# Small parameter rows and the forget gate's columns loaded on POOL's queue; every low part of w_in and u made on DVE

## The chip, the core and the metric

One core of one Trainium2 chip runs one launch of the kernel. The metric is the device time in microseconds (us), lower is better. The engines named below are PE (TensorE, matrix products), DVE (VectorE), ACT (ScalarE), POOL (GpSimd) and SP (SyncE, which here only starts transfers); transfers can be started by SP, ACT and POOL and are carried out by 16 DMA engines.

## What is computed (the reference)

One layer of a decoder on 512 tokens of width 1024: an adaLN-modulated input goes through one projection into two mixers (attention with forget gates, and a gated linear recurrence, RG-LRU), then an output projection, then a mixture of 16 experts. Cut to what the change touches:

```
mod = silu(c) @ w_ada + b_ada                  # (1, 6144): shift, scale, gate, twice
u   = layer_norm(x) * (1 + sc_m) + sh_m        # (512, 1024)
proj = u @ w_in                                # (512, 2568): q, k, v, forget logits, xb, gb
attn = forgetting_attention(q, k, v, f_logit + b_f)
lru  = rg_lru_branch(xb, gb, conv_w, conv_b, w_rg, b_rg, w_ig, b_ig, lru_lambda)
mix  = concat(rms_norm(attn), rms_norm(lru)) @ w_out
x = layer_norm(alpha * x + (1 + gt_m) * mix, ln1_g, ln1_b)
x = layer_norm(alpha * x + (1 + gt_f) * moe(layer_norm(x) * (1 + sc_f) + sh_f), ln2_g, ln2_b)
```

All of it is float32. The kernel makes a float32 product from three faster ones: each operand is split into a high part (a cast to a shorter float type, on ACT) and a low part (operand minus high part, a subtraction), and `mm3` adds high*high, low*high and high*low in PSUM (lines 101 to 103).

## The kernel before

The program is one long list of steps. PE's and SP's instructions run in the order in which they are written; those of ACT, DVE and POOL are ordered by a scheduler that looks at what each step needs, and each engine then runs its list strictly in order. A transfer is an instruction in the list of the engine that starts it. The completion of transfers is counted on a few shared semaphores: eight (DMAHW0 to 7) for transfers that SP and ACT start, eight others (DMASW0 to 7) for those of POOL. They are handed out in turn, so a transfer that takes up a semaphore first waits until the one that last used it has landed.

The start of the program, up to the projection:
- c (line 166) is loaded and turned into `cb` (line 247). ACT starts the four quarters of one w_ada block, `ws2` (line 175), then `wf`, the 32 columns of w_in that hold the forget gate's (line 391, 1024 pieces of 128 bytes), then eleven loads of small parameter rows into `v64` (lines 177 to 183). SP starts the four tiles of x (line 218), then the w_ada blocks ws0, ws3 and ws1 (line 252) with the first blocks of w_in (`wi`, line 355) between them. POOL starts `bfc` (line 185) and four loads of the recurrence's gate weights `bdr` (lines 416, 417).
- `lnx` normalizes one tile of x: statistics on DVE (line 331), the reciprocal root on POOL (line 326), the normalization on DVE (line 346), then eight transposes on PE (line 350) whose results DVE and ACT copy into `xnT` (line 351). v64 is transposed as well (line 422) and copied to `vt`.
- `ada_part` multiplies c with a w_ada block (line 265, result copied by ACT to `part`, line 267), `ada_T` turns it into columns (line 318), from which DVE makes `sc1T` (line 323) and `shT` (line 321), the scale and shift of one half of the features.
- `u_half(g)` applies scale and shift to four of eight feature blocks (DVE, line 383) and splits the result into `uh` (ACT, line 384) and `ul` (line 385). `f_half` multiplies with wf (line 396), `proj_half` a first or second half of one w_in block.

w_in comes in 20 blocks of 128 columns: eight for the recurrence (columns 1544 to 2567: four `xb`, four `gb`), then four of v, then q and k. `win_load` loads one (line 355), makes its high part `whi` on ACT (line 357) and its low part `wlo` (line 358). The pairs rotate through four buffers, so the fifth block's `whi` waits until PE has used the first block. For the recurrence's blocks 3 to 8 POOL makes the low part, for all others DVE. Three blocks are begun (`NPRE_ = 3`) while the second half of u is being made; then `proj()` finishes them, the convolution of each follows on DVE (`xc`, lines 551 and 553, split on ACT and DVE into `xch` and `xcl`), and `lru_gates` multiplies it with the gate weights on PE. Later `lru_ss` adds the squares of the recurrence's output: three additions on POOL (line 623), then four products with a column of ones (line 626).

The experts' weights are loaded by SP at line 817 into buffers that earlier stages free; their matmuls fill the second half of the program.

## Time and profile before

| | |
|---|---|
| time, median of 3 runs | 678.32 us (672.58 to 680.26) |
| the profiled execution | 675.8 us, its span 674.1 us |
| PE busy | 601.3 us, 89% of the span |
| DVE, ACT, POOL busy | 463.9, 322.7, 200.4 us |
| mean granted clock of PE | 0.956 of full speed |

The span runs from the first to the last instruction. Share of time over the whole span says little here, since PE is busy nearly all the time from about 36 us on, and waits in the first 36 us and at a few seams. The views that follow are the waits (for each engine and line, who ended its idle time: total, times, longest), the timeline (start, length, engine, line, what is written from what, and in brackets the idle time before it and its releaser) and the stretches (busy time of each engine, granted clock of PE and share of the DMA engines in a window).

### The profile page before, as it was taken

To read this page: it belongs to the slowest core of one execution; us is meant where nothing else is said; L and a number is where in the kernel's file an instruction comes from. 1 tells how busy PE (TensorE), PEld (TensorE's weight loads), DVE (VectorE), ACT (ScalarE), POOL (GpSimd) and SP (SyncE) were. 2 spreads that over 40 slices of the span, in tenths; PEclk is the share of its full clock that TensorE was granted. 3 is DMA by queue.
4 is the path that set the end of the run, shared out by engine and by line. 5 is a ranking of instruction groups with operands and counts; after the bars stand their busy time and mean duration, and the time that the engine had idled before them with its cause. 6 is when DMAs were issued, how large, how long until landed. Compare 5 with 4: busy or idle time off the path is not lost.

```text
span 674.1 us, 10228 instructions
## 1 busy us (share of the span) xinstructions
PE 601.3 (89%) x3537; PEld 444.4 (66%) x3537; DVE 463.9 (69%) x731; ACT 322.7 (48%) x508; POOL 200.4 (30%) x188
## 2 busy tenths in 40 slices
PE   1687999999995999998899999999999999999960
PEld 0444777777775887888877776666667677676440
DVE  5747869954346577779698675947695876985075
ACT  0324597334234436655286464635455564562070
POOL 5436202300000000033044353535354444443013
PEclk9899899999996999997989999999999989999795
DMA  8994317797445403184789988799989999799503
GB/s 266 339 264 149 101 29 253 235 267 253 156 158 189 154 1 125 64 298 159 261 289 361 389 288 300 287 316 351 351 300 337 368 371 362 277 381 384 207 10 118
DMA packets 91394, 164.61 MB, mean 244 GB/s; under 512 B 10169, under 2 KB 30761, under 8 KB 91340
## 3 DMA queue, kind: packets, MB, share of 16 engines
q1 hardware_dynamic: 83796, 149.02, 63.3%
q0 software_dynamic: 4624, 10.52, 6.0%
q10 hardware_dynamic: 2920, 4.39, 1.9%
q8 instruction: 29, 0.48, 0.3%
q14 instruction: 25, 0.20, 0.1%
HBM read 155.54 MB, written 12.39 MB: 249 GB/s over the span
## 4 chain that ended last, share of the span: by engine, by line
PE 63%; DVE 13%; DMA 8%; issue 6%; ACT 5%; POOL 3%; ACTq 0%; DVEq 0%; POOLq 0%; SPq 0%
PE ps L102 12%; PE ps L101 12%; PE ps L103 12%; PE ps L1416 7%; PE ps L1432 3%; DVE wlo L810 2%; DMA er<-in_w_e_down_dram 2%; DMA x2d<-y,ix 2%; DMA er<-in_w_e_gate_dram 1%; POOL wlo L810 1%; DMA wf<-in_w_in_dram 1%; DVE tail L1751 1%; PE ps L881 1%; PE ps L318 1%; PE ps L1032 1%
## 5 line engine op out<-in xcount | busy, mean ns | idle before, releaser
L810 DVE TENSOR_TENSOR wlo<-er,whi 128x1024 fp32r<-128x1024 f32 x91 | 147.5, 1638 | 28.1 <-ACT whi L809 28.0
L809 ACT CAST whi<-er 128x1024 fp32r<-128x1024 f32 x120 | 125.3, 1050 | 70.3 <-PE ps L103 62.4
L810 POOL TENSOR_TENSOR wlo<-er,whi 128x1024 fp32r<-128x1024 f32 x29 | 74.1, 2554 | 77.8 <-ACT whi L809 77.6
L101 PE MATMUL ps<-uh,whi 128*128 128x512 f32 x160 | 65.0, 406 | 0.0
L102 PE MATMUL ps<-ul,whi 128*128 128x512 f32 x160 | 62.9, 393 | 0.0
L103 PE MATMUL ps<-uh,wlo 128*128 128x512 f32 x160 | 62.9, 393 | 0.0
L1416 PE MATMUL ps<-er,xT 128*64 128x256 f32 x512 | 61.1, 393 | 0.0
L102 PE MATMUL ps<-wlo,xth 128*128 128x512 f32 x144 | 57.3, 398 | 4.0 <-POOL wlo L810 2.7
L101 PE MATMUL ps<-whi,xth 128*128 128x512 f32 x144 | 58.4, 406 | 0.0
L103 PE MATMUL ps<-whi,xtl 128*128 128x512 f32 x144 | 57.0, 396 | 1.2 <-DVE xtl L98 1.2
L326 POOL TENSOR_TENSOR rA<-rA,nhalf 128x1 f32<-128x1 f32 x4 | 2.2, 549 | 166.3 <-DVE rA L915 166.3
L1416 PEld LDWEIGHTS ps<-er,xT 128*64 128x64 f32 x512 | 36.4, 141 | 21.9 <-issue 6.1
L101 PEld LDWEIGHTS ps<-uh,whi 128*128 128x128 f32 x160 | 30.5, 191 | 12.5 <-issue 3.0
L102 PE MATMUL ps<-wlo,hth 128*128 128x512 f32 x80 | 32.6, 407 | 2.5 <-DVE wlo L810 2.5
L102 PEld LDWEIGHTS ps<-wlo,xth 128*128 128x128 f32 x144 | 27.1, 188 | 11.5 <-POOL wlo L810 4.5
L102 PEld LDWEIGHTS ps<-ul,whi 128*128 128x128 f32 x160 | 30.4, 190 | 6.5 <-issue 0.5
L103 PEld LDWEIGHTS ps<-uh,wlo 128*128 128x128 f32 x160 | 30.3, 190 | 6.6
L101 PE MATMUL ps<-whi,hth 128*128 128x512 f32 x80 | 33.0, 412 | 0.0
L103 PEld LDWEIGHTS ps<-whi,xtl 128*128 128x128 f32 x144 | 27.1, 188 | 7.8 <-DVE xtl L98 1.6
L103 PE MATMUL ps<-whi,htl 128*128 128x512 f32 x80 | 32.2, 402 | 0.0
L357 ACT CAST whi<-wi 128x1024 fp32r<-128x1024 f32 x20 | 20.9, 1047 | 22.1 <-DMA wi<-in_w_in_dram 15.5
L101 PEld LDWEIGHTS ps<-whi,xth 128*128 128x128 f32 x144 | 27.1, 188 | 5.6
(406 smaller groups left out, 1279.2 us busy)
## 6 DMA issues: line engine op xcount, KB each, us to landing
er<-in_w_e_gate_dram SPq DMA_DIRECT2D x64, 512.0 KB
er<-in_w_e_up_dram SPq DMA_DIRECT2D x64, 512.0 KB
er<-in_w_e_down_dram SPq DMA_DIRECT2D x64, 512.0 KB
wa<-in_w_ada_dram SPq DMA_DIRECT2D x44, 512.0 KB
wi<-in_w_in_dram SPq DMA_DIRECT2D x20, 512.0 KB
wo<-in_w_out_dram SPq DMA_DIRECT2D x8, 512.0 KB
wa<-in_w_ada_dram ACTq DMA_DIRECT2D x4, 512.0 KB
x<-in_x_dram SPq DMA_DIRECT2D x4, 512.0 KB
```

The lines of the kernel that those rows point to most:

```text
L101: T.matmul(o, l[0], r[0], start=start, stop=False)
L102: T.matmul(o, l[0], r[1], start=False, stop=False)
L103: T.matmul(o, l[1], r[0], start=False, stop=stop)
L318: T.matmul(p[:, b:b + 1], part[:, b * 128:(b + 1) * 128], s4 if sel_ is None else sel_, start=True, stop=True)
L357: A.copy(hl[0], r)
L809: A.copy(hl[0], r)
L810: (eng or V).tensor_sub(hl[1], r, hl[0].bitcast(F32))
L881: T.transpose(p[:, n, j, :], src[:, kb * 128:(kb + 1) * 128], ident)
L1032: T.matmul(pls[qi], yTs[qi][k // 4][:, k % 4, :], wr[:, k, :], start=k == 0, stop=k == 7)
L1416: T.matmul(p[64 * h:64 * h + 64, :], xT[:, k, :], ws[w0 + k // 2][:, k % 2, h * 256:(h + 1) * 256], start=k == 0, stop=k == 7)
L1432: T.matmul(py[64 * h:64 * h + 64, :], hT[:, k % 2, (k // 2) * 64:(k // 2) * 64 + 64], ws[8 + k][:, h * 512:(h + 1) * 512], start=k == 0, s ...
L1751: return lambda: V.scalar_tensor_tensor(ys[t][:, hs[h]], ys[t][:, hs[h]], d["r", t], g2[:, hs[h]], op0=OP.mult, op1=OP.mult)
```

## The change

1. The eleven loads into v64 and the load of wf are started by POOL instead of ACT.
2. All low parts of w_in blocks, and all low parts of u, are made on DVE: POOL loses six of 128 by 1024 and two of 128 by 512.
3. Both products `ada_part(ws3)` and `ada_part(ws1)` are issued before either `ada_T`.
4. `lru_ss` makes two additions on POOL, not three; the fourth square goes through PE, which makes eight products, not four.

```
@@ small parameters
-    A.dma_start(v64[0:8], ln1_g.rearrange("o (k p) -> (o k) p", p=128))
-    A.dma_start(v64[80:88], ln1_b.rearrange("o (k p) -> (o k) p", p=128))
+    G.dma_start(v64[0:8], ln1_g.rearrange("o (k p) -> (o k) p", p=128))
+    G.dma_start(v64[80:88], ln1_b.rearrange("o (k p) -> (o k) p", p=128))
...
     for r0, src in ((40, conv_b), (44, b_rg), (48, b_ig), (52, lru_lambda), (56, g_attn), (60, g_lru)):
-        A.dma_start(v64[r0:r0 + 4], src.rearrange("o (k p) -> (o k) p", p=128))
-    A.dma_start(v64[24:40], conv_w.rearrange("o w (k p) -> (o w k) p", p=128))
+        G.dma_start(v64[r0:r0 + 4], src.rearrange("o (k p) -> (o k) p", p=128))
+    G.dma_start(v64[24:40], conv_w.rearrange("o w (k p) -> (o w k) p", p=128))
@@ win_load
-        (V if c0 in LOV or not whl else G if 1536 <= c0 else V).tensor_sub(hl[1], r, hl[0].bitcast(F32))
+        V.tensor_sub(hl[1], r, hl[0].bitcast(F32))
@@ u_half
-            (G if k in (5, 7) else V).tensor_sub(ul[:, k, :], xnT[:, k, :], uh[:, k, :].bitcast(F32))
+            V.tensor_sub(ul[:, k, :], xnT[:, k, :], uh[:, k, :].bitcast(F32))
@@
-    A.dma_start(wf, w_in[0, :, 1536:1568].rearrange("(k p) n -> p k n", p=128))
+    G.dma_start(wf, w_in[0, :, 1536:1568].rearrange("(k p) n -> p k n", p=128))
@@
-    ada_T(3, ada_part(ws3))
-    ada_T(1, ada_part(ws1))
+    part3, part1 = ada_part(ws3), ada_part(ws1)
+    ada_T(3, part3)
+    ada_T(1, part1)
@@ lru_ss
-        for i in range(1, 4):
+        for i in (1, 2):
             G.tensor_add(lb[:, 0, :], lb[:, 0, :], lb[:, i, :])
         ssL = ps([128, 4])
         for t in range(NT):
-            T.matmul(ssL[:, t:t + 1], lb[:, 0, t * 128:(t + 1) * 128], ones1, start=True, stop=True)
+            for i in (0, 3):
+                T.matmul(ssL[:, t:t + 1], lb[:, i, t * 128:(t + 1) * 128], ones1, start=i == 0, stop=i == 3)
```

The order of the instructions moves at three places. SP's first transfers, with the semaphore that each waits for; x_190 to x_193 are the four tiles of x, wa_216 is the first quarter of ws0. Before:

```order
L218 DMA x_190<-in_x_dram 128x1024
L218 DMA x_191<-in_x_dram 128x1024 [waits DMAHW4_49]
L218 DMA x_192<-in_x_dram 128x1024 [waits DMAHW5_49]
L218 DMA x_193<-in_x_dram 128x1024 [waits DMAHW1_49]
L252 DMA wa_216<-in_w_ada_dram 128x2x512 [waits DMAHW5_49]
```

And now:

```order
L218 DMA x_190<-in_x_dram 128x1024
L218 DMA x_191<-in_x_dram 128x1024
L218 DMA x_192<-in_x_dram 128x1024
L218 DMA x_193<-in_x_dram 128x1024 [waits DMAHW0_49]
L252 DMA wa_216<-in_w_ada_dram 128x2x512 [waits DMAHW1_49]
```

DMAHW4 was the semaphore of wf; DMAHW0 and 1 are those of the first two quarters of ws2. The second and third tile of x now wait for nothing.

POOL's list from its first transfer to the first reciprocal root (rs_280). Before:

```order
L185 DMA bfc<-in_b_f_dram 8x1
L210 MEMSET mneg_178 128x128
L414 MEMSET bdr_254 128x512
L211 AFFINE_SELECT mneg_178<-mneg_178 128x128 [waits Pool_49]
L416 DMA bdr_254<-in_w_rg_dram 64x4x64 [waits Pool_49]
L417 DMA bdr_254<-in_w_rg_dram 64x4x64
...
L1026 TENSOR_TENSOR keybT<-keybT,ecol 16x1 [waits Pool_49]
L326 TENSOR_TENSOR rs_280<-ve_278,nhalf 128x1 [waits DVE_49]
```

And now; ahead of the first row stand the first eight loads into v64, which wait for nothing, and the "..." hides the last two of them:

```order
L182 DMA v_145<-in_g_attn_dram 4x128 [waits DMASW0_49]
...
L185 DMA bfc<-in_b_f_dram 8x1 [waits DMASW3_49]
L210 MEMSET mneg_178 128x128
L391 DMA wf<-in_w_in_dram 128x8x32 [waits DMASW4_49]
L211 AFFINE_SELECT mneg_178<-mneg_178 128x128 [waits Pool_49]
L414 MEMSET bdr_254 128x512
L414 MEMSET bdr_258 128x512
L416 DMA bdr_254<-in_w_rg_dram 64x4x64 [waits DMASW5_49,Pool_49]
L417 DMA bdr_254<-in_w_rg_dram 64x4x64 [waits DMASW6_49]
L416 DMA bdr_258<-in_w_ig_dram 64x4x64 [waits DMASW7_49,Pool_49]
L417 DMA bdr_258<-in_w_ig_dram 64x4x64 [waits DMASW0_49]
L326 TENSOR_TENSOR rs_280<-ve_278,nhalf 128x1 [waits DVE_49]
```

Seventeen transfers stand ahead of rs_280 where five stood, and from the ninth on each waits for an earlier one to land. DVE's list moves with it: its four casts of mneg (line 214), which need the AFFINE_SELECT, and the statistics of all four tiles of x now stand ahead of the first normalization (line 346).

DVE's list from the gate weights' low parts (bdl) to the low part of the first convolution (xcl_581). Before:

```order
L98 TENSOR_TENSOR bdl_645<-bdr_254,bdh_644 128x512
L530 TENSOR_SCALAR f_542<-ps_540,bfc 8x512
L98 TENSOR_TENSOR bdl_649<-bdr_258,bdh_648 128x512
L551 TENSOR_SCALAR xc_575<-xb_572,vt 128x512
L553 SCALAR_TENSOR_TENSOR xc_575<-xb_572,vt,xc_575 128x512 x3
L98 TENSOR_TENSOR xcl_581<-xc_575,xch_580 128x512
```

And now; wlo_587, wlo_617 and wlo_673 are the low parts of the fifth, sixth and seventh block of w_in:

```order
L98 TENSOR_TENSOR bdl_645<-bdr_254,bdh_644 128x512
L531 TENSOR_SCALAR f_542<-ps_540,bfc 8x512
L98 TENSOR_TENSOR bdl_649<-bdr_258,bdh_648 128x512
L358 TENSOR_TENSOR wlo_587<-wi_584,whi_586 128x1024
L552 TENSOR_SCALAR xc_575<-xb_572,vt 128x512
L554 SCALAR_TENSOR_TENSOR xc_575<-xb_572,vt,xc_575 128x512 x2
L358 TENSOR_TENSOR wlo_617<-wi_614,whi_616 128x1024
L554 SCALAR_TENSOR_TENSOR xc_575<-xb_572,vt,xc_575 128x512
L358 TENSOR_TENSOR wlo_673<-wi_670,whi_672 128x1024
L98 TENSOR_TENSOR xcl_581<-xc_575,xch_580 128x512
```

Three low parts now stand between the first convolution's steps, and on ACT the seventh block's `whi` stands ahead of `xch_580`, behind which it stood.

## Rows read from the trace of the kernel before

**Rows 1.** The waits of PE by line, first for 0 to 60 us, then for 60 to 130 us (total us, times, longest us).
```profile
PE ps L265 <- DVE cb L247: 11.2, 1, 11.2
...
PE ps L101 <- ACT xch L97: 3.4, 1, 3.4
PE ps L626 <- POOL lb L623: 1.6, 1, 1.6
```

**Rows 2.** The waits of SP's queue of transfers, 0 to 70 us, then 200 to 420 us.
```profile
SPq L218 <- DMA wf<-in_w_in_dram: 10.2, 1, 10.2
...
SPq L817 <- DVE wlo L747: 36.1, 3, 34.6
```

**Rows 3.** The timeline of the first 20 us: SP's four loads of x, ACT's load of wf, casts on DVE (of ident, and of mneg), POOL's first transfer, and one of DVE's statistics of x.
```profile
1.27 11.95 SPq L218 DMA_DIRECT2D x<-in_x_dram  x4
...
2.95 0.83 ACTq L391 DMA_DIRECT2D wf<-in_w_in_dram  x1
...
3.36 1.75 DVE L208 CAST idh<-ident 64x128 fp32r<-64x128 f32 x3
3.57 0.77 POOL L185 DMA_DIRECT2D bfc<-in_b_f_dram  x1
...
5.76 1.77 DVE L214 CAST mnh<-mneg 64x128 fp32r<-64x128 f32 x4
...
15.23 0.69 DVE L331 BATCH_NORM_STATS2 st<-x 128x6 f32<-128x512 f32 x1 [1.41 <-DMA x<-in_x_dram]
```

**Rows 4.** The timeline from the first reciprocal root to the first half's shift: the first copy into xnT, the normalization of the last tile of x, and shT.
```profile
16.06 0.57 POOL L326 TENSOR_TENSOR rs<-ve,nhalf 128x1 f32<-128x1 f32 x1 [6.51 <-DVE ve L335]
...
18.23 0.69 DVE L351 COPY xnT<-ps 128x512 f32<-128x512 f32 x1
...
25.16 0.81 DVE L346 TENSOR_SCALAR x<-x,mv,rs 128x1024 f32<-128x1024 f32 x1 [0.81 <-POOL rs L326]
...
31.69 0.16 DVE L321 TENSOR_TENSOR shT<-ps,vt 128x4 f32<-128x4 f32 x1 [0.85 <-PE ps L318]
```

**Rows 5.** POOL's transfers. First by line: count, busy us, mean ns of one issue; then from the view of the transfers: KB each and, last, the median us from issue to landing.
```profile
L1518 POOL DMA_INDIRECT x2d<-y,ix x10 | 22.4, 2241 | 20.3 <-PE ps L1416 7.8 <-DVE y L1517 7.1 <-DVE c L1319 3.3
...
L417 POOL DMA_DIRECT2D bdr<-in_w_ig_dram x1 | 0.6, 615 | 0.0
...
u2d<-u POOLq DMA_DIRECT2D x4, 512.0 KB, 3.2
...
xg<-u2d,ix POOLq DMA_INDIRECT x17, 8.1
...
bdr<-in_w_rg_dram POOLq DMA_DIRECT2D x2, 64.0 KB, 6.0
...
bfc<-in_b_f_dram POOLq DMA_DIRECT2D x1, 0.0 KB, 5.4
```

**Rows 6.** The timeline of PE from the product with ws3 to the first gate product: the two products (L265) and their turns into columns (L318), the first matmuls of the second block, of the finishing halves, and the second gate product (L102 with xcl).
```profile
39.62 1.92 PE L265 MATMUL ps<-wa,cb 128*32 128x512 f32 x16
42.27 1.05 PE L318 MATMUL ps<-s,part 128*128 128x1 f32 x8 [0.73 <-ACT part L267]
...
46.86 0.48 PE L101 MATMUL ps<-uh,whi 128*128 128x512 f32 x1
...
55.36 0.50 PE L101 MATMUL ps<-uh,whi 128*128 128x512 f32 x1
...
63.43 0.39 PE L103 MATMUL ps<-uh,wlo 128*128 128x512 f32 x1
...
67.97 0.50 PE L102 MATMUL ps<-xcl,bdh 128*128 128x512 f32 x1 [0.22 <-DVE xcl L98]
```

**Rows 7.** The timeline of low parts and of DVE beside them: a low part on DVE, one on POOL, scale and shift of the second half, two first steps of a convolution, and a high part with its split on ACT and DVE.
```profile
29.61 1.23 DVE L358 TENSOR_TENSOR wlo<-wi,whi 128x1024 fp32r<-128x1024 f32 x1 [1.67 <-ACT whi L357]
...
46.92 2.39 POOL L358 TENSOR_TENSOR wlo<-wi,whi 128x1024 fp32r<-128x1024 f32 x1 [9.86 <-ACT whi L357]
...
47.24 3.73 DVE L383 TENSOR_SCALAR xnT<-xnT,sc1T,shT 128x512 f32<-128x512 f32 x4
...
59.75 2.25 DVE L551 TENSOR_SCALAR xc<-xb,vt 128x512 f32<-128x512 f32 x1 [1.07 <-ACT xb L549]
...
66.58 0.62 ACT L97 CAST xch<-xc 128x512 fp32r<-128x512 f32 x1 [4.14 <-DVE xc L553]
...
67.10 1.04 ACT L357 CAST whi<-wi 128x1024 fp32r<-128x1024 f32 x1
67.23 0.69 DVE L98 TENSOR_TENSOR xcl<-xc,xch 128x512 fp32r<-128x512 f32 x1 [0.69 <-ACT xch L97]
67.84 0.54 DVE L551 TENSOR_SCALAR xc<-xb,vt 128x512 f32<-128x512 f32 x1
```

**Rows 8.** The sum of squares: POOL's last two additions in the timeline, and PE's four products in the chain that ended last (start, us, what; eight records for four products).
```profile
116.22 3.82 POOL L623 TENSOR_TENSOR lb<-lb 128x512 f32<-128x512 f32 x2 [1.50 <-ACT lb L615]
...
120.10 1.05 PE ps L626 x8
```

**Rows 9.** Stretches: busy time of PE, PEld, DVE, ACT and POOL, granted clock of PE, share of the DMA engines, GB/s.
```profile
20.00:30.00 10.00, 7.08 (x48) 4.83 (x46) 6.30 (x16) 2.95 (x6) 4.37 (x17) 0.83 1.07 368
...
70.00:72.00 2.00, 2.00 (x6) 1.60 (x5) 1.93 (x3) 0.00 (x0) 0.61 (x1) 0.50 1.12 314
...
440.00:480.00 40.00, 38.74 (x261) 26.09 (x257) 22.99 (x28) 17.36 (x22) 13.66 (x7) 1.00 1.00 331
```

More of the change, by code (lines that the diff above doesn't have):

```diff
@@ L176, in block_kernel @@
     v64 = t2k([88, 128], name="v64")
-    A.dma_start(v64[0:8], ln1_g.rearrange("o (k p) -> (o k) p", p=128))
-    A.dma_start(v64[80:88], ln1_b.rearrange("o (k p) -> (o k) p", p=128))
-    A.dma_start(v64[8:24], b_ada[0, 0:2048].rearrange("(k p) -> k p", p=128))
-    A.dma_start(v64[64:80], b_ada[0, 3072:5120].rearrange("(k p) -> k p", p=128))
+    G.dma_start(v64[0:8], ln1_g.rearrange("o (k p) -> (o k) p", p=128))
+    G.dma_start(v64[80:88], ln1_b.rearrange("o (k p) -> (o k) p", p=128))
+    G.dma_start(v64[8:24], b_ada[0, 0:2048].rearrange("(k p) -> k p", p=128))
+    G.dma_start(v64[64:80], b_ada[0, 3072:5120].rearrange("(k p) -> k p", p=128))
     for r0, src in ((40, conv_b), (44, b_rg), (48, b_ig), (52, lru_lambda), (56, g_attn), (60, g_lru)):
-        A.dma_start(v64[r0:r0 + 4], src.rearrange("o (k p) -> (o k) p", p=128))
-    A.dma_start(v64[24:40], conv_w.rearrange("o w (k p) -> (o w k) p", p=128))
+        G.dma_start(v64[r0:r0 + 4], src.rearrange("o (k p) -> (o k) p", p=128))
+    G.dma_start(v64[24:40], conv_w.rearrange("o w (k p) -> (o w k) p", p=128))
     bfc = const([8, 1], F32, "bfc")
```

## Prediction

> **What bounds the kernel now.** I read the stretches first. PE is the engine to follow: from about 36 us on it is busy nearly all the time, and in the experts' part, where the DMA engines are full too (a share of 1.00), it is busy 38.74 of 40 us at full clock [rows 9]. So I went to PE's own waits, because time comes out of this kernel only where PE waits, or where PE's work changes. Ahead of 60 us PE waits 11.2 us for `cb`; between 60 and 130 us it waits 3.4 us for the first convolution's `xch` and 1.6 us for POOL's sum of squares [rows 1]. Why the start is slow stands in the waits of SP's queue: the second load of x stood 10.2 us behind the landing of `wf` [rows 2]. The semaphore in SP's order says how: wf held the one that the second tile of x needs. So the four loads of x, which could have been started by 3 us, took until 13 us to start, and DVE's statistics waited for x at 15.23 [rows 3]. The last tile is normalized at 25.16 and the first half's shift is ready at 31.69 [rows 4]; everything up to the projection hangs on that. The reader is to see that this start isn't short of bandwidth but of early issue.
>
> The sum is made against the profiled execution: 675.8 us, of which 674.1 are the span. The median of the three runs shown is 678.3, 2.5 us more.
>
> **Part 1, the loads on POOL: the start, -4.4 us.** x no longer waits for wf. x and ws2 are 4.2 MB, and at the 368 GB/s that the DMA engines reach a little later [rows 9] they need 11.4 us, so x is there by about 14 us, against more than 15 us for its second tile alone before. But POOL now issues seventeen transfers ahead of the first reciprocal root. I follow its train. It begins at 3.6 us, where bfc is issued now. One issue takes 0.62 to 0.77 us [rows 3, 5]; I take 0.65. Eight are through at 8.8. The ninth waits for the first to land, 5.4 us after its issue as bfc did, or 6.0 as the w_rg halves did [rows 5]: with 5.7 it goes at 9.3, the twelfth ends at 11.9, and wf (it waits for the fifth load, issued at 6.2) ends at 12.6. The AFFINE_SELECT follows (0.3 us, my estimate from its neighbours), so DVE's four casts of mneg, which took 1.77 us [rows 3], run until about 14.7. Three statistics of 0.69 [rows 3] and four small steps, 0.7 together by estimate, bring 17.4. POOL meanwhile has two fills and four more loads, about 3.7 us, and is free for the roots at about 16.6. So the first normalization starts near 17.4, where one started at 16.06 + 0.57 = 16.6 before, but now all four tiles are at hand: three normalizations of 0.81 and one copy of 0.69 [rows 4] put the start of the last tile's at 20.5, and I take 20.7, since wf has 1024 pieces and bdr only 256. From there to the shift I leave the 6.5 us that it takes now (25.16 to 31.69): 25.16 - 20.7 = 4.4 us. ACT has two more instructions in that piece (an exponential and the first block's high part), which fit beside PE's last transposes and the product with ws0.
>
> Bounds: if transfers land in 3.2 us, as u2d did, the train runs without waits, and 4.9 us come back. If they need 8.1, as the gathers did, 2.4 us go again; and if wf's issue costs 2.24 us, as the scatter did [rows 5], 1.6 more: 0.4 us. The rows lie near the middle: the v loads have 4 to 16 pieces, and bfc with 8 is their nearest row. The transposition of v64 on PE needs conv_w, issued by 11.3 and landed by 17, ahead of the first tile's transposes; wf lands before 20 and is used after 27. ws2 now shares the DMA engines with x and lands later, but its column product isn't needed before the shift. These three are hidden, and bare only if the train is over 8 us late.
>
> On this train the Trainium skill speaks against the change: its page "SBUF — State Buffer", section "Who interferes with whom", says that descriptors of a transfer issued by GpSimd can't be written while VectorE runs a copy, cast or tensor_scalar in a two-port mode, and that such a DMA belongs on the ACT or SP queue. By that rule the train would come later by as much as DVE's casts overlap it, which is the first rival below. The trace doesn't bear it out in the issues: bfc's took 0.77 us, from 3.57 on, while DVE's casts of ident ran from 3.36 to 5.11 [rows 3]; in the landing times it may be contained.
>
> **Part 3, both products first, -1.65 us.** From the product with ws3 to the second block's first matmul PE takes 46.86 - 39.62 = 7.24 us; in it stand two waits for ACT's copy, the first of 0.73 us [rows 6]. In the new order one product covers the copy of the other: two times 1.85 and two times 0.95 are 5.6 us. ws1 must be there 2 us earlier than now, seen from the product with ws3; PE doesn't wait for a transfer there today. If it does then, the gain is nil.
>
> **Part 2, low parts on DVE.** DVE gets six of 1.23 us and two of about 0.65, 8.7 us; POOL loses six of 2.39 [rows 7] and the two of u. While POOL worked, DVE's own steps stretched: four scale-and-shift steps took 3.73 us and the first step of a convolution 2.25, where one takes 0.54 [rows 7]. DVE thus gets back about as much as it takes on. On PE's path I see two places. First, the third block's low part now stands on DVE behind four scale-and-shift steps (2.2 us undisturbed): with shT's 0.16, the handing over and its own 1.23 it ends some 3.8 us behind PE's last turn into columns, and PE wants it 14 matmuls of 0.23, 3.2 us, behind that: **+0.6 us** (bounds 0 and one whole low part, 1.2). Second, the seam behind the three begun blocks. Now it is 55.36 to 67.97 = 12.6 us to the second gate product [rows 6]. Afterwards: 8.4 us of matmuls (36 of 0.23, 55.36 to 63.8), then the seventh block's high part, which now stands ahead of `xch` and must wait for them, 1.04, its low part 1.23, and xcl 0.69 [rows 7]: 11.4 us. **-1.2 us** (bounds: -2.3 if that low part isn't in the way, +1.2 if the sixth's is as well). The convolution itself is done before that. The cover for the other low parts is PE's 8.4 us of matmuls, and later its unbroken run of blocks.
>
> PE's clock is at 0.50 in 70 to 72 us, behind this wait [rows 9]. With the shorter wait that may stay away, worth 1.0 us in these 2 us; it still waits some 2.5 us, so I take nothing.
>
> **Part 4, the sum of squares, -0.55 us.** POOL's last addition took 1.9 us (half of 3.82), PE waited 1.6 us for it [rows 1, 8], and the wait goes, since the second addition ends by 117.9 and PE comes at 118.5. Four more products cost PE another 1.05 us [rows 8]. (Bounds: -0.55, and +1.05 if PE comes later than POOL anyhow.)
>
> **Sum:** 4.4 + 1.65 - 0.6 + 1.2 + 0.55 = 7.2 us; 675.8 - 7.2 = 668.6, and I say 669. Added up at their worst the bounds give a loss of some 2 us, at their best a gain of 10.7.
>
> **Rivals.**
> - *The train is late.* Landing and wf at their upper bounds: part 1 gives 0.4 and the rest 2.8, 672.6 us. Or DVE's casts keep POOL from writing transfers out: those of ident from 3.57 to 5.11 and those of mneg, 1.54 + 1.77 = 3.3 us [rows 3], which leaves part 1 with 1.1: 671.9 us. For it: seventeen transfers, nine of which wait for earlier ones, with the DMA engines busier than now. Against it: the issues' durations. Chance 0.2.
> - *Slower.* Each of POOL's issues costs as much as a scatter's, 2.24 us instead of 0.65: the train ends 27 us later, and the start hangs on it: about 695 us; with half that surcharge it is 682. It decides from 7.2 / 17 = 0.42 us more for each issue, 1.07 us. Against it: no plain transfer of POOL's has taken over 0.77 us. Chance 0.07.
> - *DVE becomes the bound of the seam.* Low parts stand in order on DVE and wait for ACT's high parts, ahead of the convolution. If the sixth block's is late as well, the seam gives +1.2 instead of -1.2: 671 us. For it: three of them between four convolution steps. Chance 0.1.
> - *Nothing stays.* The experts' part has full DMA engines [rows 9]; if its loads ran free of the rest, an earlier start would be waited away: 675 us. Against it: the experts' loads wait for buffers that computation frees, 36.1 us for a low part on DVE alone [rows 2], so they move with it. Chance 0.03.
>
> **How the numbers follow.** The forecast, 4.5 to 10.5 us less (665 to 671), has 0.6. The range takes in the late train, the seam and nothing kept: 664 to 675.5. It leaves out the slower case and a little at the lower end. One per cent, 6.8 us, is about what a measurement of this kernel can tell from no change. The forecast's centre lies just beyond it, so a bit over half of its 0.6 and of its upper end, together 0.44, is faster by over 1%; the rest of it, the late train, the seam and nothing kept are within 1%, 0.49; slower 0.07.
>
> **What would show it.** SP's loads of x issued by about 3 us, the third without waiting for wf; POOL's roots at 16.5 to 17.5 us; the last normalization near 20.7 and shT near 27.3 instead of 31.69; no wait for `part` between the two turns into columns; PE's wait for `xch` and xcl down to some 2.5 us; no wait at the sum of squares, with sixteen records there. I am wrong if the train's issues or landings are longer than those rows, if ACT's first high part waits for its load and holds up the copies into xnT, or if PE's clock falls in a new place.

## The result, and the profile after

| kernel | median us (range, runs) | against the kernel before, same chip | profiled execution, its span |
|---|---|---|---|
| before | 676.47 (672.58 to 682.03, 18) | | 675.80, 674.1 |
| changed | 671.36 (667.72 to 676.90, 18) | 0.9917 [0.9897, 0.9937] | 673.18, 671.4 |
| changed, again, on another chip | 667.57 (665.86 to 668.96, 6) | 0.9857 [0.9819, 0.9895] | 666.69, 665.0 |

The change makes the kernel 0.8% faster in the first series and 1.4% in the second: 5.6 and 9.7 us by the ratios. The forecast was 669.0 in 664 to 675.5. The two intervals don't meet; whether the chip made the second gain larger isn't shown.

The waits of PE in the changed kernel, first 0 to 60 us, then 60 to 130 us (total us, times, longest):

```profile
PE ps L265 <- DVE cb L247: 5.0, 1, 5.0
...
PE ps L318 <- ACT part L267: 2.5, 1, 2.5
...
PE ps L101 <- ACT xch L97: 1.4, 1, 1.4
```

Against [rows 1], the wait for `cb` has fallen from 11.2 to 5.0 us, the seam's from 3.4 to 1.4, with 0.8 for xcl (below), and the wait for POOL's sum of squares is gone. The wait for `cb` fell because ACT's steps for c no longer stand among the eleven loads (its copy of c comes at 4.50 us instead of 12.47); it doesn't set the start now, since the first transposes still wait 1.5 us for the normalization. One wait has appeared: 2.5 us for `part` at the first half's turn into columns. The timeline of the start shows why (start, us, engine, line, operation, in brackets the idle time ahead and what ended it):

```profile
1.27 3.73 SPq L218 DMA_DIRECT2D x<-in_x_dram  x4
...
3.57 0.78 POOL L177 DMA_DIRECT2D v<-in_ln_g_dram  x1
...
9.24 0.52 POOL L182 DMA_DIRECT2D v<-in_g_attn_dram  x1 [1.22 <-DMA v<-in_ln_g_dram]
...
16.72 3.36 POOL L326 TENSOR_TENSOR rs<-ve,nhalf 128x1 f32<-128x1 f32 x4
...
20.56 0.80 DVE L346 TENSOR_SCALAR x<-x,mv,rs 128x1024 f32<-128x1024 f32 x1
...
24.75 1.04 ACT L357 CAST whi<-wi 128x1024 fp32r<-128x1024 f32 x1 [1.97 <-DMA wi<-in_w_in_dram]
25.70 1.07 ACT L351 COPY xnT<-ps 128x512 f32<-128x512 f32 x2
26.65 0.60 ACT L267 COPY part<-ps 128x512 f32<-128x512 f32 x1
27.30 1.86 PE L318 MATMUL ps<-s,part 128*128 128x1 f32 x8 [2.47 <-ACT part L267]
...
29.21 0.16 DVE L321 TENSOR_TENSOR shT<-ps,vt 128x4 f32<-128x4 f32 x1 [2.15 <-PE ps L318]
```

x is issued by 5.0 us, later than the 3 that I gave, because its fourth tile waits 2.0 us for a quarter of ws2. POOL's train ends in time for the roots at 16.72, and the last normalization starts at 20.56, both as forecast (16.5 to 17.5; 20.7). Then ACT stands 1.97 us at the first w_in block's load. Behind that high part, in ACT's order, are the last two copies into xnT and the copy of the product with ws0, for which PE waits. So shT comes at 29.21, not 27.3. PE's later places:

```profile
34.60 0.50 PE L101 MATMUL ps<-uh,whi 128*128 128x512 f32 x1
...
37.54 3.64 PE L265 MATMUL ps<-wa,cb 128*32 128x512 f32 x32
41.11 1.95 PE L318 MATMUL ps<-s,part 128*128 128x1 f32 x16
42.92 0.48 PE L101 MATMUL ps<-uh,whi 128*128 128x512 f32 x1
...
61.59 0.50 PE L101 MATMUL ps<-xch,bdh 128*128 128x512 f32 x1 [1.43 <-ACT xch L97]
62.93 0.50 PE L102 MATMUL ps<-xcl,bdh 128*128 128x512 f32 x1 [0.84 <-DVE xcl L98]
...
111.71 1.84 PE L628 MATMUL ps<-ones,lb 128*128 128x1 f32 x16
113.42 0.63 PE L641 MATMUL ps<-ident,vT 128*128 128x128 f32 x4
...
133.03 1.05 PE L290 MATMUL ps<-wa,cb 128*32 128x512 f32 x4
134.28 1.05 PE L290 MATMUL ps<-wa,cb 128*32 128x512 f32 x4 [0.20 <-DMA wa<-in_w_ada_dram]
```

Granted clock of PE in two stretches (the last three columns of a row are clock, DMA share, GB/s):

```profile
26.00:34.00 8.00, 5.47 (x15) 2.51 (x16) 5.12 (x10) 3.75 (x8) 5.81 (x12) 0.58 1.09 367
68.00:72.00 4.00, 4.00 (x19) 3.25 (x18) 3.23 (x5) 2.34 (x4) 0.00 (x0) 1.00 0.01 2
```

The half clock that stood behind the seam before (0.50 in 70 to 72 us, [rows 9]) isn't there. Behind the long wait at the first turn there is one now: that turn takes 1.86 us where it took 1.05. In PE's order, by how much the changed kernel is ahead of the kernel before: 2.0 us at the first block (36.63 to 34.60), 3.9 at the second (46.86 to 42.92), 3.7 at the product that sums the forget gate's columns (54.40 to 50.74, line 528), 5.0 at the second gate product (67.97 to 62.93), and 7.6 at the first transposes of v behind the sum of squares (121.01 to 113.42; called the turn below). There the forecast's whole sum, 7.2, had come in, though not from the places that it named. The wait for w_ada's load at the product near 134 takes 1.2 back, 6.4 are left at 142 us, and the span ends 2.7 us earlier.

### The profile page after: what moved, and what is told of

The parts are those of the page before. It is cut to its first block, busy times and chain, and to the rows that moved or that the text cites. A ratio compares the mean times of both kernels' runs of the same rounds, so it can differ in the third digit from the quotient of the medians.

```text
span 671.4 us, 10247 instructions
## 1 busy us (share of the span) xinstructions
PE 604.4 (90%) x3545; PEld 443.9 (66%) x3545; DVE 460.7 (69%) x739; ACT 322.5 (48%) x508; POOL 186.4 (28%) x191
## 4 chain that ended last, share of the span: by engine, by line
PE 66%; DVE 12%; DMA 9%; ACT 6%; issue 4%; POOL 2%; ACTq 0%; SPq 0%; DVEq 0%; POOLq 0%
PE ps L101 12%; PE ps L102 12%; PE ps L103 12%; PE ps L1418 9%; DMA wa<-in_w_ada_dram 4%; PE ps L1434 3%; DVE wlo L812 3%; DMA er<-in_w_e_down_dram 2%; DMA wi<-in_w_in_dram 2%; PE ps L290 2%; DVE tail L1753 1%; PE ps L883 1%; DMA er<-in_w_e_gate_dram 1%; PE ps L318 1%; ACT pr L861 1%
## 5 line engine op out<-in xcount | busy, mean ns | idle before, releaser
L102 PE MATMUL ps<-ul,whi 128*128 128x512 f32 x160 | 62.5, 391 | 0.0
L102 PE MATMUL ps<-wlo,xth 128*128 128x512 f32 x144 | 57.8, 401 | 5.0 <-POOL wlo L812 3.7
L358 DVE TENSOR_TENSOR wlo<-wi,whi 128x1024 fp32r<-128x1024 f32 x20 | 25.5, 1275 | 17.6 <-ACT whi L357 17.6
L102 PEld LDWEIGHTS ps<-wlo,xth 128*128 128x128 f32 x144 | 27.6, 192 | 12.6 <-POOL wlo L812 5.4
L102 PEld LDWEIGHTS ps<-ul,whi 128*128 128x128 f32 x160 | 30.1, 188 | 6.4 <-issue 0.5
L102 PE MATMUL ps<-wlo,hth 128*128 128x512 f32 x80 | 31.9, 399 | 2.6 <-DVE wlo L812 2.6
```

What stands on the lines that cost most here:

```text
L102: T.matmul(o, l[0], r[1], start=False, stop=False)
L358: V.tensor_sub(hl[1], r, hl[0].bitcast(F32))
```

## The experiments

One table for the places, in us, from each profile's timeline: the last normalization of x, shT, the first matmul of the first and of the second block, the second gate product, the turn behind the sum of squares (PE's first transposes of v), and the span.

| kernel profiled | last norm. | shT | 1st block | 2nd block | gate | turn | span | time against before |
|---|---|---|---|---|---|---|---|---|
| before | 25.16 | 31.69 | 36.63 | 46.86 | 67.97 | 121.01 | 674.1 | |
| part 2 alone | 26.52 | 32.74 | 37.70 | 47.92 | 67.96 | 118.84 | 671.3 | 0.9980 [0.9953, 1.0008] |
| part 3 alone | 27.62 | 35.41 | 40.53 | 48.85 | 69.96 | 122.98 | 673.4 | 0.9988 [0.9955, 1.0021] |
| part 4 alone | 27.31 | 34.15 | 39.10 | 49.28 | 70.39 | 122.91 | 677.4 | 1.0003 [0.9969, 1.0037] |
| wf alone | 24.96 | 31.31 | 36.26 | 46.45 | 67.56 | 120.61 | 673.7 | 0.9990 [0.9971, 1.0010] |
| v64 alone | 21.99 | 28.84 | 33.84 | 44.03 | 65.14 | 118.21 | 672.7 | 0.9999 [0.9961, 1.0036] |
| part 1 alone | 20.39 | 29.12 | 34.38 | 44.57 | 65.68 | 119.70 | 674.5 | 0.9948 [0.9913, 0.9983] |
| changed | 20.56 | 29.21 | 34.60 | 42.92 | 62.93 | 113.42 | 671.4 | 0.9917 [0.9897, 0.9937] |
| changed, again | 20.40 | 29.39 | 34.71 | 43.05 | 63.03 | 113.45 | 665.0 | 0.9857 [0.9819, 0.9895] |
| changed without part 4 | 20.45 | 28.43 | 33.84 | 42.19 | 62.20 | 113.27 | 671.1 | 0.9872 [0.9829, 0.9915] |
| first w_in block ahead | 21.97 | 29.79 | 34.74 | 43.08 | 62.78 | 114.75 | 671.1 | 0.9955 [0.9930, 0.9981] |
| start reordered | 24.07 | 34.07 | 39.55 | 47.91 | 67.61 | 117.83 | 677.2 | 0.9994 [0.9965, 1.0023] |
| casts late | 20.58 | 28.81 | 35.16 | 44.11 | 63.77 | 115.72 | 673.8 | 0.9923 [0.9892, 0.9955] |
| casts late, again | 20.31 | 27.92 | 33.40 | 41.77 | 61.44 | 113.50 | 669.1 | 0.9875 [0.9830, 0.9921] |

**The four parts one by one**, each made alone in the kernel before; the edits are the hunks of the diff above. For parts 2 to 4 the interval takes in no change, so the places decide.

> Part 1 alone: the fifteen parameter loads' issues of v64 and wf on POOL, all else as before. Theory (the start's gain is real, but ACT's first high part of w_in waits for its load and holds up the copies into xnT, and PE passes the place at half clock): the last normalization starts at 20.5 to 21 us as in the changed kernel (20.56) against 25.16 before, but shT is written near 29.2, that is 2 to 2.5 us earlier than before, not 4.4; the first w_in block's high part waits about 2 us for its load; the first matmul of the second block's projection stands some 2 us earlier than before; total -2 to -2.5 us. Rival (the step from the last normalization to shT was lengthened by one of the other parts): shT near 27.3 and a total of -4.4 us.

Part 1 (twelve loads, not fifteen): as the theory said for the wait and shT (29.12), with 8.73 us from the last normalization to shT without the other parts; the total, 3.5 us [1.2, 5.9], lies between theory and rival and can't tell them apart. The table says why. The last normalization of the profile before, 25.16, was an early one: with the same start the runs of parts 2, 3 and 4 have it at 26.52 to 27.62 and the first block at 37.70 to 40.53. Over the four executions with the old start the first block begins at 38.49 on average, over the four with the new one (part 1, changed twice, without part 4) at 34.38: 4.1 us, although each of the four carries the new wait. With the old start spread over 3.9 us and the new one over 0.9, that is known to a microsecond or two.

> Part 2 alone: all low parts of w_in and u on DVE. Theory: the third block's low part is later (PE there +0.3 us), the seam behind the three begun blocks is shorter by 1.4 us, and if the wait for xch and xcl falls well below its 3.4 us, PE's stretch of half clock behind it (68.8 to 72.2 us) goes too, another -1.6 us; at 90 us PE stands 2.5 to 3 us earlier than before, and the total is -2.5 to -3 us. Rival (the clock there came back only because the whole start was different): half clock stays behind the seam, and the total is -0.9 to -1.1 us. Second rival (DVE is the bound): the seam is longer, total +0.5 to +1.5 us.

Part 2: from the second block to the forget gate's product (line 528) 7.84 us instead of 7.54 (+0.3); from there to the second gate product 12.20 instead of 13.57 (-1.4). PE's row at the seam and the stretch behind it, for part 2 alone:

```profile
66.61 0.50 PE L101 MATMUL ps<-xch,bdh 128*128 128x512 f32 x1 [1.43 <-ACT xch L97]
...
64.00:72.00 8.00, 5.73 (x25) 4.14 (x24) 6.84 (x9) 2.67 (x4) 0.20 (x2) 1.00 1.07 360
```

and the stretch for part 1 alone, which has the long wait of 3.4 us:

```profile
64.00:72.00 8.00, 7.05 (x17) 5.36 (x18) 6.46 (x8) 2.66 (x4) 2.60 (x3) 0.57 0.80 267
```

Full clock with the short wait, half clock with the long one. That is so in all six profiles with the 3.4 us wait, and in five of the eight with the short one; in three others (first block ahead, and both of casts late) half clock comes there all the same. Where it stays away PE gains another 1.6 us: the changed kernel goes from 5.0 us ahead at the gate product to 6.6 in the blocks behind it, where it waits for nothing. From its first block to the last matmul ahead of the sum of squares part 2 alone took 78.75 us where the kernel before takes 81.46, 2.7 less, where the theory had 2.5 to 3. Its own start was 1.1 us later, and its time (-1.4 us, uncertain by 1.9) can't tell the theory from its first rival.

Before, `xch` waited for the convolution [rows 7]. What holds the seam now ACT and DVE of the changed kernel show:

```profile
59.97 1.04 ACT L357 CAST whi<-wi 128x1024 fp32r<-128x1024 f32 x1 [1.19 <-PE ps L102]
60.92 0.61 ACT L97 CAST xch<-xc 128x512 fp32r<-128x512 f32 x1
...
61.05 1.23 DVE L358 TENSOR_TENSOR wlo<-wi,whi 128x1024 fp32r<-128x1024 f32 x1 [0.29 <-ACT whi L357]
62.19 0.68 DVE L98 TENSOR_TENSOR xcl<-xc,xch 128x512 fp32r<-128x512 f32 x1
```

The seventh block's high part waits for PE and stands ahead of `xch`, its low part ahead of xcl, as the prediction had it; the convolution is done by then.

> Part 3 alone: both column products before their turns into columns. Theory: from the product with ws3 to the second block's first matmul PE takes 1.7 to 1.9 us less than the 7.24 us of before, nothing downstream gives it back ahead of the gate, total -1.7 us. Rival: the product with ws1 is now early and waits for its load, or the transposes wait for ACT's second copy: 0 to -0.5 us.

Part 3: from the first block's first matmul to the second's 8.32 us instead of 10.23: -1.9, and 10.2 in every kernel without it. Settled for the place; the time of the run (-0.8 us, uncertain by 2.2) can't tell it from its rival.

> Part 4 alone: two additions on POOL, eight small products on PE. Theory: PE's wait of 1.6 us for POOL's last addition goes, four products more cost up to 1 us: 0.5 to 1.8 us earlier behind it (the changed kernel showed -0.8 from the row ahead of it to the last of the products, with the wait gone); and since the start isn't earlier here, the loads of w_ada that follow are as far along as before, so that the product with w_ada some 20 us later waits at most 1 us for its load. Total -0.5 to -1 us. Rival: all of it is waited away at the w_ada products, total 0.

Part 4: the wait went, and from the last matmul ahead to the turn PE took 1.94 us instead of 2.92, so -1.0. The expectation for w_ada's load was missed: PE waited for it though the start wasn't early, and was later by 1.6. The total is nil within 2.3 us, which takes in theory and rival.

**Which move frees x.** The edit is the one hunk on wf, or the one on v64's rows.

> The kernel before with one load moved: wf on POOL, the eleven rows of v64 left on ACT. Theory: SP's loads of x wait because ACT's and SP's loads take the same few completion semaphores in turn, so that whatever stands in the turn ahead is waited for; in the order of this kernel the second tile of x then has the semaphore of the fourth load of ws2, and is started at 7 to 9 us, when that has landed, instead of 12.6; shT 30 to 31 us, total -1 to -2.5 us. Rival (wf with its 1024 pieces is the whole cause): the second load of x starts by 2 us as in the changed kernel, the train on POOL is short, last normalization 18 to 20 us, shT 27 to 29, total -3 to -5 us.

> The kernel before with the eleven rows of v64 on POOL, wf left on ACT. Theory (the turn of the semaphores): with the rows out of the turn the first loads of x meet fresh semaphores although wf stands where it stood; x is issued by 5 to 6 us, the last normalization is at 19.5 to 20.6 and shT at about 29 as in the run with all loads moved, total -2 to -4 us: the eleven rows do the work and moving wf adds nothing. Rival (wf itself): the second load of x still waits 10 us for wf, POOL's train holds the roots until 15.5 us besides, total 0 to +1 us.

SP's waits in the first 30 us (queue and line, what it waited for, total us, times, longest), wf alone:

```profile
SPq L218 <- DMA wa<-in_w_ada_dram: 8.8, 1, 8.8
```

and v64 alone:

```profile
SPq L218 <- DMA wa<-in_w_ada_dram: 6.7, 2, 3.7
...
SPq L252 <- DMA wf<-in_w_in_dram: 1.8, 1, 1.8
```

With wf gone, x waits 8.8 us for a quarter of ws2, which it neither reads nor overwrites. So the turn of the semaphores is the cause, and wf was only what stood in it. The second load went at about 10.5 us (11.9 before), later than the 7 to 9 that I gave, and the first block came 0.4 us earlier, which is within the spread of the old start. The v64 rows alone let x out by 9.5 us and bring shT to 28.84, without the move of wf and with x behind two quarters of ws2; the 5 to 6 us that I expected for x is missed. The load that waits for wf is now the third quarter of ws0, started at 15.65. In time neither run is clear of no change.

**Where the lost 1.9 us of the start went.**

> The changed kernel with SP's first w_in block issued ahead of the four loads of ws0. Theory (ACT's first high part waited 1.97 us for that block and held up the last two copies into xnT and, behind them, the copy that PE's first half's turn into columns waited 2.47 us for): the wait for wi goes, PE's wait for part at that turn falls to 0.7 to 1.0 us, and shT comes at 27.3 to 28 instead of 29.21; PE may wait up to 1.4 us for ws0, which now lands behind 0.5 MB more. Against the changed kernel's 671.4 us that is -1 to -2 us, 669.5 to 670.5. Rival (ws0 is what lands last anyhow): PE waits as long at the product with ws0 as it did at the turn, shT stays at 29 or later, 671 to 673 us.

```diff
-    ws0 = ada_load(0, RAW)
     w_ahead()
+    ws0 = ada_load(0, RAW)
```

The wait for that load went, and from the product with ws0 to shT it took 3.75 us (26.04 to 29.79) where the changed kernel takes 6.30 (22.91 to 29.21). But nothing was won: the time, 673.4 us, is near the rival's, by another way than it gave. With the block there early, its low part ran on DVE ahead of the normalizations:

```profile
18.06 1.22 DVE L358 TENSOR_TENSOR wlo<-wi,whi 128x1024 fp32r<-128x1024 f32 x1 [0.70 <-ACT whi L357]
19.20 2.25 DVE L346 TENSOR_SCALAR x<-x,mv,rs 128x1024 f32<-128x1024 f32 x3
...
```

PE then waited 3.6 us for the first of them, and its transposes ran at half clock (0.50 in 20 to 22 us): the first eight took 1.97 us instead of 1.09, and the product with ws0 began 3.1 us later.

> The run before this one with POOL's queue put in another order besides: mneg's fill and select ahead of the loads of v64, the four loads of bdr behind the first block's projection, and the turn of v64 behind all four tiles' transposes. Theory (POOL's train, not x, held the roots in the changed kernel: x's last tile was issued by 5.0 us and the first root ran at 16.72): the first root runs at 13.5 to 14 us, the last normalization at 16.5 to 18 instead of 20.56, and the start is then held by the landing of ws0, near 22 us; shT 26 to 27.5, 667.5 to 669.5 us. Rival (x lands late and the train hid it): the last normalization stays at 20 or later with a wait for x ahead of the third or fourth statistics, no more than the run before this one gives.

```diff
+    mneg = t2k([128, 128], name="mneg")
+    G.memset(mneg, 0.0)
+    G.affine_select(mneg, mneg, pattern=[[-1, 128]], compare_op=OP.is_ge, fill=-1e30, base=0, channel_multiplier=1)
     v64 = t2k([88, 128], name="v64")
...
     lnx(0)
-    pst = ps()
-    T.transpose(pst[:, 0:88], v64, ident[0:88, 0:88])
-    V.tensor_copy(vt, pst[:, 0:88])
     lnx(1)
-    ada_T(2, part)
     lnx(2)
     lnx(3)
+    pst = ps()
+    T.transpose(pst[:, 0:88], v64, ident[0:88, 0:88])
+    V.tensor_copy(vt, pst[:, 0:88])
+    ada_T(2, part)
```

(and the loop that makes bdr stands behind `proj_half(0, 0)`). The roots did run early, at 13.35 us, but DVE took the third tile's statistics behind its copies out of PSUM, and the last normalization fell to 24.07. PE waited 3.7 us for it and then ran the whole stretch to 32 us at half clock:

```profile
22.00:32.00 10.00, 8.84 (x41) 5.75 (x41) 4.07 (x11) 1.38 (x3) 3.35 (x15) 0.50 1.07 370
```

Both expectations missed.

> The changed kernel with ACT's high part of the first w_in block put behind the four copies into xnT and the copy of the column product with ws0 (the second and third block's behind the first half of u as now). Nothing else in the start moves; one tiny copy is added. Theory (the wait for that block's load, standing in ACT's queue ahead of the copies, is what kept 1.9 of the predicted 4.4 us from coming back): the last copy into xnT ends at about 24.6 instead of 26.7, PE's wait for part at the first half's turn falls from 2.5 to 0.7 us, shT comes at 27.0 to 27.6 instead of 29.21, the first block's first matmul 1.5 to 2 us earlier than 34.60; 0.5 to 2 us less than the run of the changed kernel beside it. Rival (ws0's load or PE's clock holds that place too): shT at 28.5 or later, within 0.5 us of the changed kernel.

```diff
-        A.copy(hl[0], r)
-        V.tensor_sub(hl[1], r, hl[0].bitcast(F32))
+        if len(whl) > 2:
+            w_split(r, hl)
+        else:
+            first.append((r, hl))
...
     part = ada_part(ws0)
+    A.copy(first[0][1][0][:, 0, 0:4], part[:, 0:4])
+    w_split(*first[0])
     ada_T(0, part)
     u_half(0)
+    w_split(*first[1])
+    w_split(*first[2])
```

(`w_split` holds the two lines taken out.) ACT and PE in the start of this kernel:

```profile
25.18 0.59 ACT L351 COPY xnT<-ps 128x512 f32<-128x512 f32 x1 [0.29 <-PE ps L350]
27.09 0.59 ACT L267 COPY part<-ps 128x512 f32<-128x512 f32 x1 [1.32 <-PE ps L265]
27.93 1.04 ACT L366 CAST whi<-wi 128x1024 fp32r<-128x1024 f32 x1
...
18.36 1.97 PE L350 MATMUL ps<-ident,x 128*128 128x128 f32 x8 [1.18 <-DVE x L346]
20.27 1.91 PE L350 MATMUL ps<-ident,x 128*128 128x128 f32 x8
...
25.07 1.92 PE L265 MATMUL ps<-wa,cb 128*32 128x512 f32 x16
27.73 1.05 PE L318 MATMUL ps<-s,part 128*128 128x1 f32 x8 [0.73 <-ACT part L267]
```

The mechanism is shown: no wait for the load, 0.73 us for `part`, and from the product with ws0 to shT 3.74 us (25.07 to 28.81) where the changed kernel takes 6.30 and 6.65 in its second profile. That is 2.6 to 2.9 us. Part of it is PE's clock: in the run without part 4 (below) ACT waits the same way, but the turn itself runs at full clock:

```profile
27.34 1.05 PE L318 MATMUL ps<-s,part 128*128 128x1 f32 x8 [2.61 <-ACT part L267]
```

There the stretch takes 5.63 us (22.80 to 28.43). So the wait alone costs 1.9 us, and the half clock that follows it in the other three profiles with this wait 0.8 more (the turn takes 1.86 or 1.87 us there instead of 1.05). But the sixteen transposes ahead took 1.97 and 1.91 us instead of 1.09 and 1.04, so the product began 2.2 us later and the rival's number, 28.81, came out. The time, 672.04 us, is above the 667.57 of the changed kernel beside it, where I had expected it below. Once more:

> The kernel with the casts of the first w_in block behind the copies, once more. In its first profile the wait for part was 0.7 us as foretold, and from the product with ws0 to shT it took 3.74 us instead of 6.30; but the first sixteen transposes of x took 1.97 and 1.91 us where the changed kernel's took 1.09 and 1.04, so the product with ws0 began 2.2 us later. Theory (that slower stretch of PE is a matter of the single execution, as its place differs between profiles of like starts): this time the transposes take about 1.1 us each, the product with ws0 begins at 22.7 to 23.1, shT comes at 26.5 to 27.0, and the time is 0.5 to 2 us below the changed kernel's, 666 to 670.5 us. Rival (the slow stretch belongs to this order of ACT's work): transposes at 1.9 us again, shT at 28.5 or later, 670.5 to 673 us.

The transposes took 1.97 and 1.66 us, as the rival had it; from the product with ws0 to shT it took 3.74 us again; shT came at 27.92, between the two. The time, 669.44 us, is within the theory's range, but 1.9 above the changed kernel's on that chip. In the three profiles where ACT's wait is gone and the tiles keep their order (first block ahead, casts late twice) the first transposes took 1.97 us; in the four that have it, 1.09. That is PE's half clock, on record in two of the three. Casts late, again:

```profile
18.00:20.00 2.00, 1.91 (x10) 1.91 (x11) 1.87 (x4) 0.00 (x0) 1.89 (x5) 0.50 1.06 351
```

First block ahead has 0.50 under its transposes too, the four with ACT's wait have 1.00. For the first run of casts late 1.00 is recorded as well, but its transposes took as long (see the last section). PE's rows ahead of that place hardly differ between casts late and the changed kernel, so whether the half clock there is chance or comes with the order stays open. None of these versions is faster than the changed kernel clear of noise, and start reordered is slower (0.9994 [0.9965, 1.0023] against 0.9917 [0.9897, 0.9937]).

**What the second half of the kernel does to the total.**

> The changed kernel itself once more, so that its profile is a second sample and the two runs after it stand beside it on one chip. Theory (what was given back behind 300 us in the first profile, from 6.3 to 2.7 us, is where the half-clock stretches happened to fall): up to 142 us the places repeat within 0.5 us (shT at 29.2, waits for xch and xcl 1.4 and 0.8, no wait at the sum of squares, a wait for w_ada's load at the product at 134), while the number and places of half-clock stretches behind 300 us differ, and with them 1 to 3 us. Rival (the give-back belongs to the change): the same stretches at the same places. Time 669 to 673 us either way.

Up to the turn behind the sum of squares the two executions of the changed kernel agree within 0.2 us. Then three stretches, cut at the same products of PE, from the first one with the attention's output (at) to the tail, in the first execution (stretch and its length, busy time of PE first, clock third from the end):

```profile
256.19:320.85 64.66, 59.69 (x394) 53.51 (x392) 50.78 (x137) 31.75 (x83) 12.49 (x23) 0.89 0.56 199
320.85:358.29 37.44, 32.33 (x211) 26.46 (x211) 30.01 (x63) 22.87 (x28) 14.34 (x10) 0.95 0.79 276
...
407.65:642.97 235.32, 227.34 (x1341) 154.48 (x1339) 160.90 (x184) 112.91 (x139) 92.83 (x47) 0.99 0.92 323
```

and the same work in the second:

```profile
254.97:318.28 63.31, 58.33 (x394) 52.02 (x392) 50.81 (x137) 31.70 (x83) 12.47 (x23) 0.92 0.55 192
318.28:354.42 36.14, 32.06 (x210) 26.46 (x211) 29.95 (x63) 22.86 (x28) 14.07 (x10) 0.95 0.87 301
...
403.79:636.00 232.21, 225.63 (x1341) 154.12 (x1339) 159.90 (x184) 112.89 (x139) 93.70 (x47) 0.99 0.94 328
```

The same program is 1.35 + 1.30 + 3.11 = 5.8 us apart here, by its granted clock and by its waits for low parts (7.5 against 6.1 us in the last stretch). So what the first profile gave back behind 256 us is not the change's. The kernel before, cut at the same products, takes 384.4 us from the first stretch to the last, the changed kernel 386.8 and 381.0. The wait for w_ada near 134 us, which I expected again, didn't come back, and the time, 667.57 us, is below the 669 to 673 that I gave.

> The changed kernel without its last part: three additions on POOL and four products on PE for the sum of squares, as before. Theory (what part 4 gives at the sum of squares is waited away at the product with w_ada some 20 us later, since the load there is then late): PE waits 1.2 to 1.6 us for POOL's last addition, doesn't wait for the load of w_ada at the product near 134 us, and behind 142 us PE stands within 0.3 us of the changed kernel; the time is that of the changed kernel within 0.5 us. Rival (the gain of part 4 stays): PE stands 0.8 us or more later behind 142 us, and the time is 0.5 to 1.2 us longer.

```diff
-        for i in (1, 2):
+        for i in range(1, 4):
...
-            for i in (0, 3):
-                T.matmul(ssL[:, t:t + 1], lb[:, i, t * 128:(t + 1) * 128], ones1, start=i == 0, stop=i == 3)
+            T.matmul(ssL[:, t:t + 1], lb[:, 0, t * 128:(t + 1) * 128], ones1, start=True, stop=True)
```

PE's rows at the sum of squares without part 4:

```profile
112.36 1.05 PE L627 MATMUL ps<-ones,lb 128*128 128x1 f32 x8 [1.09 <-POOL lb L624]
113.27 0.64 PE L640 MATMUL ps<-ident,vT 128*128 128x128 f32 x4
```

From the gate product to the turn 51.07 us against 50.49 and 50.42 with part 4; from the last matmul ahead of the sum to the turn 2.39 against 1.94. So it gives 0.5 to 0.6. The theory that this is always waited away at w_ada's product fell: of seven profiles with part 4, three pay 1.2 to 1.6 us more there (changed, part 4 alone, start reordered), of seven without it, one pays 1.1 (v64 alone). That leans to part 4 but doesn't settle it. In time the run can't be told from the changed kernel.

## Why the prediction came out, and where it didn't

- **Part 1, x without wf and the train on POOL: right to the last normalization** (20.56 for 20.7). That the Trainium skill's rule in "SBUF — State Buffer", section "Who interferes with whom", would hold the train up by 3.3 us isn't borne out: the issues of v64 took 0.50 to 0.78 us, and the roots began at 16.72.
- **The step that failed** is "From there to the shift I leave the 6.5 us that it takes now", with ACT's extra instructions that "fit beside". It took 8.65 us: the high part of the first block has come ahead of two copies in ACT's order, and its load lands later than ACT arrives. ACT's 1.97 us cost PE 1.9 us, and PE's clock fell behind that wait, so that the turn took 1.86 us instead of 1.05. The 6.5 us weren't a clean figure either: in the profile before, PE stood at 0.57 of its clock in 24 to 28 us, and the last eight transposes took 1.89 us. Against the profile that I worked from the start gave 2.5 us at shT and 2.0 at the first block, not 4.4. By the four executions of either start it is worth 4.1 us at the first block: the profile before happened to have the earliest of the four old starts.
- **Part 3:** -1.9 for -1.65. Both waits for ACT's copy went, as the sum had it; the two products took 3.57 us to the first turn where I had 3.7, the two turns 1.81 where I had 1.9.
- **Part 2:** +0.3 for +0.6, -1.4 for -1.2, a wait of 2.27 us for "some 2.5". The clock behind the seam, for which I took nothing and had 1.0 as the prize, gave 1.6 in both profiles of the changed kernel; it isn't certain to. That is luck in the sum below.
- **Part 4:** -1.0 in the pair of profiles for -0.55. Four products more cost 0.8 us (1.71 to the turn against 0.91), not 1.05; and where part 2 is made the wait was only 1.09 (both profiles; 1.20 to 1.97 in the five with neither part), so that 0.5 to 0.6 is left for part 4 itself.
- **A term that was missing: the end.** POOL's last drain (an instruction at the end of its list) grows with its transfers. The drain of the kernel before, of wf alone, v64 alone and of the changed kernel (the last of the three durations, in ns, is the long one):

```profile
L1873 POOLq DRAIN  x3: 46/103/3505, 669.7 to 673.8; - x3
```

```profile
L1873 POOLq DRAIN  x3: 46/103/3587, 669.3 to 673.5; - x3
```

```profile
L1873 POOLq DRAIN  x3: 46/103/4403, 667.5 to 672.4; - x3
```

```profile
L1875 POOLq DRAIN  x3: 46/103/4485, 666.1 to 671.2; - x3
```

  One, eleven and twelve transfers more make it 0.08, 0.90 and 0.98 us longer. All engines wait for it at the end: in the kernel before it is over at 673.25 us, SP's own at 670.96. So 1.0 us of the gain goes back there. (From the tail's first product to the end of the span the changed kernel takes 28.43 us, and 29.00 in its second profile, the one before 27.17; the rest of that is ahead of the drain and differs from one execution to the next.) I followed POOL's transfers only to the roots.
- **The sum.** 7.6 us at the turn behind the sum of squares for 7.2 forecast is luck in part: the start gave 2.0 for 4.4, and 1.6 of clock, for which I took nothing, made up for most of that; part 3 gave 1.9, part 2 1.1 (1.4 less 0.3), part 4 1.0. Behind it the first profile loses 1.2 at w_ada's load, 2.4 between 256 and 643 us and 1.3 in the tail, which leaves 2.7; in the second the middle gains 3.4 and the tail loses 1.8, which leaves 9.1. The series give 5.6 and 9.7. How much of that gap is chip and how much chance no run separates: casts late, measured twice on one chip, gave 672.04 and 669.44.
- **The chances.** Of the rivals, the late train, the slow issues and DVE as the seam's bound didn't happen, and some of the gain stayed. "ACT's first high part waits for its load and holds up the copies into xnT, or PE's clock falls in a new place" stood only in the list of what would make me wrong, with no price; both happened.

## What to carry to other kernels

When a wait ahead of a stage goes, look at every instruction in the in-order queues behind it for a load that used to be early enough, and price it: here a 1.97 us wait of ACT for a block that nothing needed yet cost PE 1.9 us, and 0.8 more where its clock fell behind the wait. Taking the wait out can be paid for elsewhere: none of the three versions without it ran faster. A load's semaphore can wait for a transfer that has nothing to do with it; moving small loads to another queue renews the whole turn. And POOL pays for transfers that it takes over again when it is drained at the end.

## What the runs showed of the hardware

- POOL's drain at the end grew by 0.08 us with each further transfer (3.505 us with 42, 3.587 with 43, 4.403 with 53, 4.485 with 54), for wf with its 1024 pieces as much as for a row of v64.
- The granted clock doesn't always tell PE's speed: in the first run of casts late the sixteen transposes took 1.97 and 1.91 us in a stretch whose granted clock is 1.00 throughout, in the changed kernel's second profile 1.09 and 1.04 at the same figure:

```profile
18.00:22.00 4.00, 3.64 (x18) 3.64 (x19) 3.48 (x7) 0.59 (x1) 3.52 (x9) 1.00 1.06 309
```

  In casts late, again, the first eight took 1.97 us as well, and there 0.50 is recorded (the row in the section on the lost 1.9 us). So the first run was at 1.2 instead of 2.4 GHz too, by these times, without a record of it. The Trainium skill says in "TensorE: Matmul & The Clock Gate", section "Seeing it yourself", that recorded clock events have been seen to be unreliable on this chip; these rows agree with it, and by them a stretch's clock is better read from the length of its matmuls.
- Two executions of one program differ by 5.8 us between 256 and 643 us with the same work, so a change of some 5 us can be read from a profile only by place, ahead of there.
